# Out stage of a hybrid decoder layer: casts, low halves and sums of the output product ordered behind the newest convolution instruction of their engine

## The chip, the cores and the metric

The kernel runs on 1 core of one Trainium2 chip. The metric is the device time of the whole program in microseconds; each measurement is one execution, and the time before is the median of 3 of them. The core's engines are named as the profile names them: PE (matrix products), DVE, ACT and POOL (element-wise work), SP (issues DMAs); each works off its own stream of instructions in the order in which the compiler put them.

## What is computed

One layer of a decoder over 2048 prompt tokens and 8 x 4 sample tokens. Four branches of 512 channels each (convolution, pooling mixer, stick-breaking attention, attention into a memory) are gated, put side by side and multiplied by `w_out`; a norm, the residual and a final norm follow. The change touches the last part, which the reference writes so:

```python
def conv_branch(a, b, hist, w_dw, b_dw, ln_g, ln_b, w_pw, b_pw):
    ...
    y = y + b_dw                          # depthwise convolution
    y = jax.nn.silu(layer_norm(y, ln_g, ln_b))
    y = y @ w_pw + b_pw
    return y, u_ext[:, -(CONV_K - 1):]

mix = jnp.concatenate([y_c * jax.nn.silu(cg), y_p * jax.nn.silu(pg),
                       y_s * jax.nn.silu(sg), y_m * jax.nn.silu(mg)], axis=-1)
out = rms_norm(mix @ w_out, post_g)
return x + out, conv_new, pool_new, k, v
```

## The kernel before

The kernel first projects the tokens, runs the sample group's attention and the depthwise convolution, then the attention of the prompt. What is left at about 1960 us is the **out stage**, in which two streams of work are woven together.

The first is the **output product** `mix @ w_out`, 2048 x 2048 by 2048 x 1024. It is done as seven block products (a scheme of the Strassen kind, products 1, 7, 2, 6, 4, 5, 3 in this order), each of which is cut into parts `(prod, i, h)`: 128 tokens of sums or differences of `mix` rows against a half `h` of the block's weights. fp32 values are split into a high and a low half that PE can take: `hi` is a cast (ACT) and `lo = value - hi` (DVE or POOL). A part is therefore 12 matmuls (line 1968): for each of four slices of 128 rows `mh x wohi`, `mh x wolo`, `ml x wohi`. The helpers of a part: `out_load` (SP issues the DMA of rows into `mr`), `out_combine` (sums or differences of rows on POOL, lines 1698, 1701 and 1705, and on DVE, line 1704), `out_high` (ACT cast `mr` -> `mh`, line 1713), `out_low` (DVE `ml`, line 1724), and for the weights `weight_high` (ACT cast `wor` -> `wohi`, line 1620) and `weight_low` (`wolo`, line 1625). `lows(...)` asks for a part's `ml` in the second of the four steps of the part three places ahead of it (`AHEAD = 4`, `LOWK = 1`).

The second stream is `conv_post`, the **rest of the convolution branch**, eight blocks of 256 tokens, named by their first token (0, 256, 512 ... 1792). A block goes through a long chain from engine to engine:

- `total`: POOL adds four channel groups to `cs` (line 1442)
- `center`: PE `cm` (mean, line 1447), DVE `cy` (line 1450), ACT `csq` (squares, line 1452), POOL adds of `csq` (line 1454)
- `scale`: PE `cv` (variance, line 1460), ACT square root (line 1461), DVE reciprocal (line 1462), then twice, for two of the four channel groups: DVE `ct` (line 1469), ACT sigmoid `csg` (line 1472), DVE `ct` (line 1476), ACT `shi` (line 1478), DVE `slo` (line 1481). Square root and sigmoid need different tables in ACT, which an ACT_TABLE_LOAD loads
- `point`: PE `cz` (line 1502), four times 12 matmuls on `shi` and `slo`, with a DVE `cgt` (line 1505) and a store of the rows of `mix` after each

`conv` is advanced by one step whenever the loop over the parts has made 0.9 of a step (`OPACE`), so both streams are traced interleaved, and products 2 and 6 take the rows that the convolution writes.

PE's instruction order is fixed to the order of the program text, by `tc.manual_schedule` for PE. On DVE, ACT and POOL the order is chosen by the scheduler of the framework: an instruction may stand ahead of one that was traced earlier, where its operands come sooner. `tc.issue_after(x)` adds an edge to what is traced inside it: the instruction is not put ahead of `x`. It carries no data.

## Time and profile before

| | us |
|---|---|
| median of 3 runs | 2381.64 (2380.49 to 2384.3) |
| the profiled execution, whole time | 2378.62 |
| its span in the profile | 2376.9 |
| PE busy in the span | 2279.8 (96%) |
| DVE busy | 1720.7 (72%) |
| POOL busy | 1277.5 (54%) |
| ACT busy | 1119.1 (47%) |

The granted clock of the core is 0.989 on average. The out stage with the convolution in it lies between about 1960 and 2180 us; what follows to the end has output product and norms alone. A row of the timeline is: start in us, duration in us, engine, line, operation, out <- in, shapes, how many in the row, and in brackets the idle time ahead of it on its engine with what ended it. A row of the table by windows has for each engine the busy time and, in brackets, the instructions, and then PEclk (the clock granted to PE, 1.00 is full speed), the share of DMA time and GB/s.

### The profile page before, as it was taken

The page shows a single profiled execution, that of the slowest core. Times are in us where ns is not written, and L with a number is a line of the kernel's source. Part 1 is how long each engine was busy: PE and PEld are TensorE (multiplying, and loading weights), DVE is VectorE, ACT ScalarE, POOL GpSimd, SP SyncE. Part 2 cuts the span into 40 slices and gives each one's busy share as a digit, 9 for nine tenths or more (in the row PEclk, how much of TensorE's full clock was granted, in tenths as well). Part 3 has the DMA queues.
Part 4 walks back from the last instruction along what each step waited for, and adds up shares of the span by engine and source line. Part 5 has one row for each costly group of instructions (what it writes and reads, how often), then busy time and mean ns, then how long its engine had stood idle before and what let it go on. Part 6 is the DMA issues. An engine that isn't in the chain of part 4 may idle for free. (4 is left out here: it accounts for less than half of the span.)

```text
span 2376.9 us, 42227 instructions
## 1 busy us (share of the span) xinstructions
PE 2279.8 (96%) x16024; PEld 1772.0 (75%) x16024; DVE 1720.7 (72%) x2428; ACT 1119.1 (47%) x1947; POOL 1277.5 (54%) x1322
## 2 busy tenths in 40 slices
PE   7999999999999999999999999899999999999996
PEld 7898888888888777777777777555555557778775
DVE  5342786969557673577777877978898956777897
ACT  5322342242442322224242425788999965444554
POOL 3554546455565546445555552799877754432230
PEclk9999999999999999999999999999999999999998
DMA  6689977878778999887877775566442207866674
GB/s 213 194 282 299 336 270 261 281 259 276 256 257 311 321 346 344 308 289 267 299 262 269 262 264 154 143 214 216 111 107 72 76 23 249 265 210 196 233 236 158
DMA packets 336868, 557.94 MB, mean 235 GB/s; under 512 B 27985, under 2 KB 212433, under 8 KB 320266
## 3 DMA queue, kind: packets, MB, share of 16 engines
q1 hardware_dynamic: 281290, 286.53, 38.8%
q0 software_dynamic: 55376, 268.72, 31.9%
q8 instruction: 126, 2.06, 0.4%
q14 instruction: 76, 0.62, 0.1%
HBM read 465.09 MB, written 90.68 MB: 234 GB/s over the span
## 5 line engine op out<-in xcount | busy, mean ns | idle before, releaser
L966 DVE STREAM_TRANSPOSE T<-kt 128x1024 f32<-128x1024 f32 x256 | 308.7, 1226 | 190.4 <-PE sSA L979 177.3
L933 POOL DMA_INDIRECT vt<-in_cache_v_dram,idv x256 | 252.4, 986 | 260.0 <-PE sO L1018 199.0
L618 DVE SCALAR_TENSOR_TENSOR cacc<-U,par,cacc 128x512 f32<-128x512 f32 x480 | 359.9, 750 | 11.0
L1344 POOL TENSOR_TENSOR be<-be,E 128x512 f32<-128x512 f32 (+3 forms) x316 | 300.7, 963 | 67.4 <-DVE E L1332 23.7
L1335 DVE TENSOR_TENSOR_SCAN E<-gam,cr,ZM 128x513 f32<-128x513 f32 x192 | 233.3, 1264 | 21.6 <-ACT gam L1266 13.5
L933 POOL DMA_INDIRECT kt<-in_cache_k_dram,idk x128 | 128.5, 1004 | 195.0 <-DVE T L966 153.2
L1355 PEld LDWEIGHTS AT<-ident,be 128*128 128x128 f32 x1082 | 117.3, 142 | 136.5 <-ACT at L1361 40.6
L1968 PE MATMUL acc<-wohi,mh 128*128 128x512 f32 (+1 forms) x480 | 193.3, 403 | 0.5 <-DVE mh L1724 0.5
L1266 ACT ACTIVATE gam<-S,nbias_bc 128x1024 f32<-128x1024 f32 (+1 forms) x158 | 170.2, 1077 | 45.3 <-ACT be L1267 15.1
L1968 PE MATMUL acc<-wolo,mh 128*128 128x512 f32 (+1 forms) x480 | 189.4, 395 | 0.0
L1968 PE MATMUL acc<-wohi,ml 128*128 128x512 f32 x448 | 177.6, 396 | 5.4 <-DVE ml L1724 5.4
L1262 PE MATMUL S<-kT,Q 128*128 128x512 f32 (+1 forms) x632 | 175.8, 401 | 4.8 <-ACT be L1267 4.8
L1355 PE MATMUL AT<-ident,be 128*128 128x128 f32 x1082 | 160.4, 284 | 20.6 <-DVE at L1359 8.7
L1267 ACT ACTIVATE be<-S,bias_bc 128x1024 f32<-128x1024 f32 (+1 forms) x158 | 169.1, 1070 | 0.4 <-DMA gsd<-sg1sg 0.4
L1371 PE MATMUL av<-at,V 128*64 128x512 f32 (+3 forms) x640 | 152.8, 557 | 3.9 <-DVE sbo L1376 3.9
L979 PE MATMUL sSA<-T,W 128*32 128x128 f32 x4096 | 139.8, 276 | 2.7 <-DVE T L966 1.4
L979 PEld LDWEIGHTS sSA<-T,W 128*32 128x32 f32 x4096 | 105.1, 109 | 37.6 <-issue 31.2
L1018 PE MATMUL sO<-vt,saT 128*32 128x512 f32 x1024 | 122.2, 592 | 0.0
L1262 PEld LDWEIGHTS S<-kT,Q 128*128 128x128 f32 x632 | 106.1, 195 | 18.4 <-ACT be L1267 5.8
L1361 ACT COPY at<-AT 128x512 f32<-128x512 f32 x192 | 108.9, 651 | 19.7 <-PE AT L1355 19.6
L1332 DVE TENSOR_TENSOR_SCAN E<-gam,ZM 128x384 f32<-128x384 f32 (+1 forms) x124 | 94.5, 811 | 32.0 <-ACT gam L1266 26.3
L1724 DVE TENSOR_TENSOR ml<-mr,mh 128x512 fp32r<-128x512 f32 x108 | 91.0, 849 | 30.8 <-ACT mh L1713 30.6
(577 smaller groups left out, 6030.2 us busy)
## 6 DMA issues: line engine op xcount, KB each, us to landing
Q<-qd SPq DMA_DIRECT2D x64, 256.0 KB
mr<-mixd SPq DMA_DIRECT2D x32, 512.0 KB
mr<-mixd SPq DMA_DIRECT2D x48, 256.0 KB
xtp<-in_x_prompt_dram SPq DMA_DIRECT2D x16, 512.0 KB
kT<-kd SPq DMA_DIRECT2D x64, 128.0 KB
ws<-in_w_out_dram SPq DMA_DIRECT2D x16, 512.0 KB
wsd<-ws SPq DMA_DIRECT2D x16, 512.0 KB
msd<-mr SPq DMA_DIRECT2D x32, 256.0 KB
```

Source lines behind the costliest of these rows:

```text
L618: dve.scalar_tensor_tensor(out=ps, in0=U[:, a + k : a + k + H], scalar=wd[:, k : k + 1], in1=ps, op0=ALU.mult, op1=ALU.add)
L933: pool.indirect_dma_start(out=dst, out_offset=None, in_=rows, in_offset=bass.IndirectOffsetOnAxis(ap=idx, axis=0))
L966: S["turn"] = dve.transpose(T[:, 2 * hh : 2 * hh + 2].rearrange("p s j t -> p (s j t)"), kt[:, 2 * hh : 2 * hh + 2].rearrange("p s j d -> ...
L979: pe.matmul(sSs[n][32 * g : 32 * g + 32, P * ml : P * (ml + 1)], lhsT=W[:, jj, :], rhs=T[:, :, jj, :], start=i == 0, stop=i == 3, tile_pos ...
L1262: pe.matmul(S[:, j, :w], lhsT=Q[:, x, P * (q2 + j) : P * (q2 + j + 1)], rhs=kt[:, :w], start=x == 0, stop=x == 1)
L1266: act.activation(out=ga, in_=S[:, :, :w], func=AF.Sigmoid, bias=nbias_bc[:, h : h + 1], scale=-1.0)
L1267: act.activation(out=be, in_=S[:, :, :w], func=AF.Sigmoid, bias=bias_bc[:, h : h + 1])
L1335: dve.tensor_tensor_scan(out=E[:, j][:, ::-1], data0=g_[:, j][:, ::-1], data1=ZM[:, 0:1].to_broadcast([P, 513]), initial=carry[hh, q2][:, ...
L1344: pool.tensor_tensor(out=be[:, j, :m], in0=be[:, j, :m], in1=E[:, j, 513 - w : 513 - w + m], op=ALU.mult)
L1355: pe.transpose(ap_[:, P * qt : P * (qt + 1)], A[hp, qb, kc, hh, qt][:, P * r : P * (r + 1)], ident)
L1371: pe.matmul(av[64 * hh : 64 * hh + 64, c], lhsT=V[:, 4 * kc + r, 64 * hh : 64 * hh + 64], rhs=ats.pop((hp, qb, kc, r, hh))[:, c], start=dg ...
L1968: pe.matmul(o[:rows], lhsT=m[a][:, k, :rows], rhs=W[prod, 4 * h + k][w], start=not cont and h == k == n == 0, stop=h == 1 and k == 3 and n ...
```

## The change

`mark()` remembers, for ACT, DVE and POOL apart, the newest instruction of `conv_post` that has been traced. `behind_conv(eng)` wraps an instruction of the output product in `tc.issue_after` of that one. So each cast, low half, sum and difference of rows and weights in the out stage is no longer put ahead of convolution work that was traced before it on the same engine. Nothing is added to or taken from the computation, and the DMAs' and PE's code is untouched. Before the first marked instruction `latest` is empty, and nothing is wrapped.

```diff
+    latest = {}
+
+    def mark(x):
+        latest[x.ins.engine] = x.ins
+        return x
+
+    def behind_conv(eng):
+        x = latest.get({id(act): mybir.EngineType.Activation, id(dve): mybir.EngineType.DVE,
+                        id(pool): mybir.EngineType.Pool}[id(eng)])
+        return tc.issue_after(x) if x is not None else ExitStack()
...
@@ scale (so marked: every ACT, DVE and POOL instruction of total, center, scale and point)
-            dve.reciprocal(out=vps[:, :N], in_=vps[:, :N])
+            mark(dve.reciprocal(out=vps[:, :N], in_=vps[:, :N]))
...
@@ weight_high, weight_low
-        act.copy(hi, ts[0])
+        with behind_conv(act):
+            act.copy(hi, ts[0])
...
-        eng.tensor_tensor(out=lo, in0=raw_, in1=hi.bitcast(F32), op=ALU.subtract)
+        with behind_conv(eng):
+            eng.tensor_tensor(out=lo, in0=raw_, in1=hi.bitcast(F32), op=ALU.subtract)
...
@@ out_combine (so too its other sums, on POOL and DVE)
-            pool.tensor_tensor(out=ts[0], in0=ts[0], in1=ts[1], op=ALU.subtract)
+            with behind_conv(pool):
+                pool.tensor_tensor(out=ts[0], in0=ts[0], in1=ts[1], op=ALU.subtract)
...
@@ out_high
-        act.copy(mh[:, :, :rows], raws[x])
+        with behind_conv(act):
+            act.copy(mh[:, :, :rows], raws[x])
...
@@ out_low
-        eng.tensor_tensor(out=lo, in0=raw_, in1=hi.bitcast(F32), op=ALU.subtract)
+        with behind_conv(eng):
+            eng.tensor_tensor(out=lo, in0=raw_, in1=hi.bitcast(F32), op=ALU.subtract)
```

On PE no instruction moves. On the others the instructions of the out stage change places. Two places show how. The names in the rows carry the block or the part: `ct768_2` is channel group 2 of convolution block 768, `ml7_5_0` the low half of part (7, 5, 0); the number behind is a running one. In the changed kernel line 1713 has become 1720, 1724 has become 1732, 1756 has become 1764, and 1620 has become 1621.

DVE before, at the variance of convolution block 768, from the end of the block before to the first `slo`:

```order
L1724 TENSOR_TENSOR ml7_5_0_21063<-mr7_5_0_20898,mh7_5_0_21062 128x512
L1505 SCALAR_TENSOR_TENSOR cgt512_3_20976<-cz512_3_20996,par_116,cgt512_3_20976 128x256
L1756 TENSOR_TENSOR U3_20131<-acc7_3_20948,U2_20130 128x512
L1462 RECIPROCAL cv768_21032<-cv768_21032 128x256
L1724 TENSOR_TENSOR ml7_5_1_21108<-mr7_5_1_20942,mh7_5_1_21107 128x512
L1469 SCALAR_TENSOR_TENSOR ct768_0_21042<-cy768_20565,par_116,cv768_21032 128x256
L1469 SCALAR_TENSOR_TENSOR ct768_1_21046<-cy768_20565,par_116,cv768_21032 128x256
L1450 TENSOR_TENSOR cy1024_20821<-cy1024_20821,cm1024_21115 128x256 x4
L1476 SCALAR_TENSOR_TENSOR ct768_0_21042<-ct768_0_21042,par_116,csg768_0_21044 128x256
L1476 SCALAR_TENSOR_TENSOR ct768_1_21046<-ct768_1_21046,par_116,csg768_1_21048 128x256
L1756 TENSOR_TENSOR U3_20131<-acc7_4_21065,U2_20130 128x512
L1481 TENSOR_TENSOR slo768_21041<-ct768_0_21042,shi768_21040 128x256
```

The same place after the change; the reciprocal, `ml7_4_1` and `ct768_0` of line 1469 stand just ahead of the first row:

```order
L1469 SCALAR_TENSOR_TENSOR ct768_1_21046<-cy768_20565,par_116,cv768_21032 128x256
L1450 TENSOR_TENSOR cy1024_20821<-cy1024_20821,cm1024_21115 128x256 x4
L1476 SCALAR_TENSOR_TENSOR ct768_0_21042<-ct768_0_21042,par_116,csg768_0_21044 128x256
L1476 SCALAR_TENSOR_TENSOR ct768_1_21046<-ct768_1_21046,par_116,csg768_1_21048 128x256
L1764 TENSOR_TENSOR U3_20131<-acc7_4_21065,U2_20130 128x512
L1481 TENSOR_TENSOR slo768_21041<-ct768_0_21042,shi768_21040 128x256
L1481 TENSOR_TENSOR slo768_21041<-ct768_1_21046,shi768_21040 128x256
L1469 SCALAR_TENSOR_TENSOR ct768_2_21071<-cy768_20565,par_116,cv768_21032 128x256
L1469 SCALAR_TENSOR_TENSOR ct768_3_21075<-cy768_20565,par_116,cv768_21032 128x256
L1476 SCALAR_TENSOR_TENSOR ct768_2_21071<-ct768_2_21071,par_116,csg768_2_21073 128x256
L1476 SCALAR_TENSOR_TENSOR ct768_3_21075<-ct768_3_21075,par_116,csg768_3_21077 128x256
L1732 TENSOR_TENSOR ml7_5_0_21063<-mr7_5_0_20898,mh7_5_0_21062 128x512
```

`ml7_5_0` stood three rows ahead of the reciprocal; it now stands behind the second pair of line 1476, so that the reciprocal, eight `ct`, four `cy` and two `slo` stand ahead of it. `ml7_5_1`, which followed the reciprocal, now follows the last `slo` of the block.

ACT before, between the square root and the sigmoid of convolution block 512:

```order
L1713 CAST mh7_2_0_20795<-mr7_2_0_20637 128x512
L1461 ACT_TABLE_LOAD
L1461 ACTIVATE cv512_20765<-cv512_20765,eps_t_93 128x256
L1713 CAST mh7_2_1_20836<-mr7_2_1_20693 128x512
L1713 CAST mh7_3_0_20876<-mr7_3_0_20746 128x512
L1620 CAST wohi2_4_21139<-wor2_4_20915 128x512
L1620 CAST wohi2_5_21178<-wor2_4_20915 128x512
L1472 ACT_TABLE_LOAD
L1472 ACTIVATE csg512_0_20777<-ct512_0_20775,par_116 128x256
L1472 ACTIVATE csg512_1_20781<-ct512_1_20779,par_116 128x256
```

The same place after the change:

```order
L1720 CAST mh7_1_1_20750<-mr7_1_1_20617 128x512
L1461 ACT_TABLE_LOAD
L1461 ACTIVATE cv512_20765<-cv512_20765,eps_t_93 128x256
L1472 ACT_TABLE_LOAD
L1472 ACTIVATE csg512_0_20777<-ct512_0_20775,par_116 128x256
L1472 ACTIVATE csg512_1_20781<-ct512_1_20779,par_116 128x256
L1478 CAST shi512_20773<-ct512_0_20775 128x256
L1478 CAST shi512_20773<-ct512_1_20779 128x256
L1720 CAST mh7_2_0_20795<-mr7_2_0_20637 128x512
L1472 ACTIVATE csg512_2_20806<-ct512_2_20804,par_116 128x256
```

The weight casts `wohi2_4` and `wohi2_5` and two row casts no longer stand between square root and sigmoid; `mh7_2_0` has moved from ahead of the square root to behind the first two `shi`.

More of the change, by code (lines that the diff above doesn't have):

```diff
@@ L1441, in total @@
                 for c in range(3):
-                    pool.tensor_tensor(out=sums[i], in0=sums[i] if c else ys[i][:, 0, :N], in1=ys[i][:, c + 1, :N], op=ALU.add)
+                    mark(pool.tensor_tensor(out=sums[i], in0=sums[i] if c else ys[i][:, 0, :N], in1=ys[i][:, c + 1, :N], op=ALU.add))
         def center(i):
@@ L1449, in center @@
             for c in range(4):
-                dve.tensor_tensor(out=y[:, c, :N], in0=y[:, c, :N], in1=mps[:, :N], op=ALU.subtract)
+                mark(dve.tensor_tensor(out=y[:, c, :N], in0=y[:, c, :N], in1=mps[:, :N], op=ALU.subtract))
                 sq.append(cp.tile([P, CW], F32, tag="csq", name=f"csq{a0}_{c}", bufs=4)[:, :N])
-                act.activation(out=sq[c], in_=y[:, c, :N], func=AF.Square)
+                mark(act.activation(out=sq[c], in_=y[:, c, :N], func=AF.Square))
             for a, b in ((0, 1), (2, 3), (0, 2)):
-                pool.tensor_tensor(out=sq[a], in0=sq[a], in1=sq[b], op=ALU.add)
+                mark(pool.tensor_tensor(out=sq[a], in0=sq[a], in1=sq[b], op=ALU.add))
             sqs[i] = sq[0]
@@ L1460, in scale @@
             pe.matmul(vps[:, :N], lhsT=ones_ln, rhs=sqs.pop(i), start=True, stop=True)
-            act.activation(out=vps[:, :N], in_=vps[:, :N], func=AF.Sqrt, bias=eps_t)
-            dve.reciprocal(out=vps[:, :N], in_=vps[:, :N])
+            mark(act.activation(out=vps[:, :N], in_=vps[:, :N], func=AF.Sqrt, bias=eps_t))
+            mark(dve.reciprocal(out=vps[:, :N], in_=vps[:, :N]))
             yield
@@ L1468, in scale @@
                     t = ps_(f"ct{a0}_{c}")[:, :N]
-                    dve.scalar_tensor_tensor(out=t, in0=y[:, c, :N], scalar=par[:, c, CONV_K + 1 : CONV_K + 2],
-                                             in1=vps[:, :N], op0=ALU.mult, op1=ALU.mult)
+                    mark(dve.scalar_tensor_tensor(out=t, in0=y[:, c, :N], scalar=par[:, c, CONV_K + 1 : CONV_K + 2],
+                                                  in1=vps[:, :N], op0=ALU.mult, op1=ALU.mult))
                     sg = cp.tile([P, CW], F32, tag="csq", name=f"csg{a0}_{c}", bufs=4)[:, :N]
-                    act.activation(out=sg, in_=t, func=AF.Sigmoid, bias=par[:, c, CONV_K + 2 : CONV_K + 3])
+                    mark(act.activation(out=sg, in_=t, func=AF.Sigmoid, bias=par[:, c, CONV_K + 2 : CONV_K + 3]))
                     ts[c] = t, sg
@@ L1475, in scale @@
                 for c, (t, sg) in ts.items():
-                    dve.scalar_tensor_tensor(out=t, in0=t, scalar=par[:, c, CONV_K + 2 : CONV_K + 3], in1=sg,
-                                             op0=ALU.add, op1=ALU.mult)
-                    act.copy(shi[:, c, :N], t)
+                    mark(dve.scalar_tensor_tensor(out=t, in0=t, scalar=par[:, c, CONV_K + 2 : CONV_K + 3], in1=sg,
+                                                  op0=ALU.add, op1=ALU.mult))
+                    mark(act.copy(shi[:, c, :N], t))
                 yield
                 for c, (t, _) in ts.items():
-                    dve.tensor_tensor(out=slo[:, c, :N], in0=t, in1=shi[:, c, :N].bitcast(F32), op=ALU.subtract)
+                    mark(dve.tensor_tensor(out=slo[:, c, :N], in0=t, in1=shi[:, c, :N].bitcast(F32), op=ALU.subtract))
             split[i] = shi, slo
@@ L1504, in point @@
                         n += 1
-                dve.scalar_tensor_tensor(out=g[:, :N], in0=ps[:, :N], scalar=par[:, co, CONV_K + 3 : CONV_K + 4],
-                                         in1=g[:, :N], op0=ALU.add, op1=ALU.mult)
+                mark(dve.scalar_tensor_tensor(out=g[:, :N], in0=ps[:, :N], scalar=par[:, co, CONV_K + 3 : CONV_K + 4],
+                                              in1=g[:, :N], op0=ALU.add, op1=ALU.mult))
                 wq.dma_start(mix_rows(co, a0, CB), by_tile(g[:, :CB]))
@@ L1697, in out_combine @@
         if prod == 5 and i < LAST:
-            pool.tensor_tensor(out=ts[1], in0=ts[0], in1=ts[1], op=ALU.add)
+            with behind_conv(pool):
+                pool.tensor_tensor(out=ts[1], in0=ts[0], in1=ts[1], op=ALU.add)
             ts = ts[1:]
         elif prod == 7:
-            pool.tensor_tensor(out=ts[0], in0=ts[0], in1=ts[1], op=ALU.subtract)
+            with behind_conv(pool):
+                pool.tensor_tensor(out=ts[0], in0=ts[0], in1=ts[1], op=ALU.subtract)
             stores.append(((0, i, h), msd[0, i, h], ts[0]))
         elif prod == 6:
-            dve.tensor_tensor(out=ts[0], in0=ts[0], in1=ts[1], op=ALU.subtract)
-            pool.tensor_tensor(out=ts[2], in0=ts[2], in1=ts[0], op=ALU.subtract)
+            with behind_conv(dve):
+                dve.tensor_tensor(out=ts[0], in0=ts[0], in1=ts[1], op=ALU.subtract)
+            with behind_conv(pool):
+                pool.tensor_tensor(out=ts[2], in0=ts[2], in1=ts[0], op=ALU.subtract)
             stores.append(((1, i, h), msd[1, i, h], ts[2]))
```

## The prediction

> **What bounds the kernel now.** I read the engines' busy time first, then what PE waits for in the out stage, then the clock by windows of 5 us, and last the timelines around two convolution blocks.

> ```profile
> span 2376.9 us, 42227 instructions
> PE 2279.8 (96%) x16024; PEld 1772.0 (75%) x16024; DVE 1720.7 (72%) x2428; ACT 1119.1 (47%) x1947; POOL 1277.5 (54%) x1322
> ```

> PE is busy 96% of the span, and its order does not change. So the change can only alter the time in which PE stands still or runs at a lower clock. These are PE's waits between 1960 and 2180 us (line waited in, whom it waits for, us in total, times, longest):

> ```profile
> PE cz L1502 <- ACT shi L1478: 9.6, 4, 4.0
> PE cz L1502 <- DVE slo L1481: 2.7, 6, 0.8
> PE acc L1968 <- DVE ml L1724: 1.9, 3, 0.8
> PE cz L1502 <- DVE cgt L1505: 1.7, 1, 1.7
> ```

> They add up to 15.9 us. Of these 14.0 are PE waiting for the convolution (`cz`), and only 1.9 are PE waiting for the low halves of the output product (`ml`). Some of the stalls also cost clock, as the windows show (PEclk is the third number from the end):

> ```profile
> 2005.00:2010.00 5.00, 1.78 (x11) 1.24 (x9) 1.64 (x5) 2.50 (x6) 0.99 (x1) 0.94 0.77 277
> 2010.00:2015.00 5.00, 4.16 (x15) 3.56 (x16) 3.84 (x9) 2.76 (x8) 3.31 (x3) 0.50 0.75 229
> 2015.00:2020.00 5.00, 5.00 (x29) 4.54 (x29) 1.12 (x3) 0.50 (x1) 4.59 (x6) 0.88 1.06 367
> 2040.00:2045.00 5.00, 3.57 (x11) 2.89 (x12) 4.79 (x8) 2.62 (x8) 4.92 (x5) 0.51 0.75 257
> 2045.00:2050.00 5.00, 5.00 (x29) 4.53 (x28) 4.12 (x5) 0.00 (x0) 4.84 (x5) 0.81 0.82 237
> 2120.00:2125.00 5.00, 3.01 (x13) 2.41 (x13) 4.40 (x11) 2.71 (x8) 2.32 (x3) 0.70 0.96 336
> 2125.00:2130.00 5.00, 5.00 (x22) 4.40 (x21) 3.72 (x7) 0.62 (x1) 3.92 (x5) 0.62 0.45 151
> ```

> Three times PE falls to about half clock after it has stood still. What that costs is the busy time times the share of the clock that is missing: 4.16 x 0.50 + 5.00 x 0.12 = 2.7 us the first time, 3.57 x 0.49 + 5.00 x 0.19 = 2.7 the second, 3.01 x 0.30 + 5.00 x 0.38 = 2.8 the third; 8.2 us in all. Waits and clock together are **24.1 us**, which is all that the change could win here.

> Why the convolution comes late is seen at block 512, on ACT and DVE:

> ```profile
> 2031.68 1.14 ACT L1620 CAST wohi<-wor 128x512 fp32r<-128x512 f32 x2 [3.24 <-DMA wor<-in_w_out_dram]
> 2032.84 1.28 ACT L1472 ACT_TABLE_LOAD   x1
> 2034.13 0.84 ACT L1472 ACTIVATE csg<-ct,par 128x256 f32<-128x256 f32 x2
> 2034.64 0.88 DVE L1476 SCALAR_TENSOR_TENSOR ct<-ct,par,csg 128x256 f32<-128x256 f32 x2 [3.50 <-ACT csg L1472]
> ```

> ACT waits 3.24 us for a weight DMA, casts, and only then gets to the sigmoid; DVE meanwhile stands still for 3.50 us. Weight casts which nothing needs soon stand ahead of a chain that PE is about to need. The change takes these out of the way; that is its gain.

> **The change part by part. The gain.** With `wohi2_4` and `wohi2_5` behind the sigmoids, the 3.24 us wait, the casts' 1.14 us and the like at the other blocks leave the chain. I also expect PE to come later to `cz` because of what follows, by some 4 us a block. Both together should end nearly all `cz` waits: 14.0 us, the 1.9 for `ml` being replaced by the term below, and the 8.2 us of clock. Gain 24.1, at least 15 if some `slo` and `cgt` waits and one low clock stay.

> **The loss.** The low halves that PE needs within the chain now stand behind it. Block 768 ran undisturbed before, so I cost it there. PE, DVE and ACT from the block's variance `cv` on:

> ```profile
> 2054.08 0.59 PE L1460 MATMUL cv<-csq,ones_ln 128*128 128x256 f32 x2
> 2061.95 0.40 PE L1968 MATMUL acc<-wohi,mh 128*128 128x512 f32 x1
> 2062.42 0.40 PE L1968 MATMUL acc<-wohi,ml 128*128 128x512 f32 x1
> 2054.72 0.45 ACT L1461 ACTIVATE cv<-cv,eps_t 128x256 f32<-128x256 f32 x1 [1.53 <-PE cv L1460]
> 2059.54 1.28 ACT L1472 ACT_TABLE_LOAD   x1 [0.19 <-DVE ct L1469]
> 2060.83 0.84 ACT L1472 ACTIVATE csg<-ct,par 128x256 f32<-128x256 f32 x2
> 2065.29 0.83 ACT L1472 ACTIVATE csg<-ct,par 128x256 f32<-128x256 f32 x2
> 2056.73 1.75 DVE L1462 RECIPROCAL cv<-cv 128x256 f32<-128x256 f32 x1
> 2058.39 0.67 DVE L1724 TENSOR_TENSOR ml<-mr,mh 128x512 fp32r<-128x512 f32 x1
> 2058.98 0.87 DVE L1469 SCALAR_TENSOR_TENSOR ct<-cy,par,cv 128x256 f32<-128x256 f32 x2
> 2060.05 1.42 DVE L1450 TENSOR_TENSOR cy<-cy,cm 128x256 f32<-128x256 f32 x4 [0.20 <-PE cm L1447]
> 2061.38 0.88 DVE L1476 SCALAR_TENSOR_TENSOR ct<-ct,par,csg 128x256 f32<-128x256 f32 x2
> 2062.89 0.76 DVE L1481 TENSOR_TENSOR slo<-ct,shi 128x256 fp32r<-128x256 f32 x2
> 2063.56 0.87 DVE L1469 SCALAR_TENSOR_TENSOR ct<-cy,par,cv 128x256 f32<-128x256 f32 x2
> 2064.34 0.69 DVE L1724 TENSOR_TENSOR ml<-mr,mh 128x512 fp32r<-128x512 f32 x1
> 2065.79 0.88 DVE L1476 SCALAR_TENSOR_TENSOR ct<-ct,par,csg 128x256 f32<-128x256 f32 x2 [0.77 <-ACT csg L1472]
> 2066.58 1.67 DVE L1724 TENSOR_TENSOR ml<-mr,mh 128x512 fp32r<-128x512 f32 x1
> 2068.17 0.74 DVE L1481 TENSOR_TENSOR slo<-ct,shi 128x256 fp32r<-128x256 f32 x2
> ```

> The matmul at 2061.95 opens accumulator `acc7_5`: it takes `mh7_5_0`, and two matmuls later, at 2062.42, PE takes `ml7_5_0`. That is 8.3 us after `cv`. After the change `ml7_5_0` stands behind the second pair of line 1476. This pair ended at 2065.79 + 0.88 = 2066.7. One `ml` (0.69 us, at 2064.34) leaves the chain ahead of it; the one behind the reciprocal is only exchanged for another. So the pair ends between 2066.0 and 2066.7, and the `ml` behind it takes 0.69 to 1.67 us (both durations are in the rows; the long ones are those beside POOL's work). So `ml7_5_0` is there at 2066.7 to 2068.4, 12.6 us or more after `cv` where PE wants it after 8.3: PE stands from 2062.4 on, for **4.3 to 6.0 us**. Its `mh7_5_0` is late as well, behind the first two `shi` on ACT, but less, so that adds nothing.

> The order shows the same at the other blocks: one low half that PE wants 7 to 8 us after `cv` stands behind the second `ct` pair or behind the last `slo` (about 0.7 us more, from the row at 2068.17). For blocks 0, 1536 and 1792 somewhat less stands ahead of it. For these I take 3 to 4 us, for the other five 4.3 to 5.7: 3 x 3.5 + 5 x 4.8 = **34.5 us** over eight blocks; ends 8 x 3.0 = 24 (ends of chains tighten everywhere) and 8 x 5.7 = 46.

> PE cannot make up for this: what it lacks is the next part in its fixed order. The helpers behind the late `ml` (`ml7_5_1` after the last `slo`, then `wolo`) have a part's 12 matmuls as cover, 2.8 us, which about holds; if that cover is gone, each costs the 0.69 us of one more `ml`, inside the upper end.

> **Clock.** The long waits ahead of the three low clocks:

> ```profile
> 2010.82 0.58 PE L1502 MATMUL cz<-shi,pwhi 128*128 128x256 f32 x1 [4.04 <-ACT shi L1478]
> 2040.65 0.58 PE L1502 MATMUL cz<-shi,pwhi 128*128 128x256 f32 x1 [3.29 <-ACT shi L1478]
> 2042.01 0.58 PE L1502 MATMUL cz<-slo,pwhi 128*128 128x256 f32 x1 [0.78 <-DVE slo L1481]
> 2122.31 0.58 PE L1502 MATMUL cz<-shi,pwhi 128*128 128x256 f32 x1 [1.67 <-ACT shi L1478]
> ```

> 4.04 us in one piece, 3.29 and 0.78 in two, and once only 1.67 us at the end of a stretch with several short waits. The new stalls lie at 3 to 5.7 us, so more than half should set it off: 4.5 times 2.7 = **12 us**, ends 1 x 2.7 and 8 x 2.7 = 22. [...]

> **Costed at nothing.** The weight casts and lows pushed back (`wohi`, `wolo`, 24 each): `wohi2_4` is cast at 2031.68, and at 2061.95 PE only opens `acc7_5`, ahead of product 2 by six parts of 2.8 us (twelve matmuls at the 0.235 us between 2061.95 and 2062.42), so product 2 cannot begin before 2078; these 46 us hide a delay of one or two chains (13 us each); if that cover were gone it would be one more stall of the kind above. POOL's sums (mean 1.49 us, row below) wait mostly for DMA and stand three parts ahead; behind POOL's `csq` sums they are a chain late at most, and SP's stores of their results with them. The DMA issues on SP keep their places but for buffers freed later.

> ```profile
> L1701 POOL TENSOR_TENSOR mr<-mr 128x512 f32<-128x512 f32 x16 | 23.7, 1488 | 42.4 <-DMA mr<-mixd 27.7 <-DVE ct L1476 6.2 <-DVE ml L1724 4.5
> ```

> Bounds for these together: 0 and 8 us. From the end of the convolution on, nothing is marked any more and the orders agree.

> **The sum** against the profiled execution, 2378.6 us: - 24.1 + 34.5 + 12 = +22.4, so 2401 us; that execution lies 3.0 us below the median of the runs (2381.64 - 2378.62), so **2404 us**, 0.9% slower.

> **The rivals.** *A, faster: the low halves are in time.* Place: DVE between the reciprocal and the second `ct` pair. If the chain from `cv` to that pair took less than the 8.3 us after which PE asks for `ml`, every stall would go: 2381.6 - 24.1 = 2358 us. For it: part of the chain is waiting (3.50 us at block 512, 1.53, 0.77 at 768), and ACT has fewer instructions in between. Against it: the chain's own work, each step waiting for the one before, is 0.59 + 0.45 + 1.75 + 0.87 + 1.28 + 0.84 + 0.88 + 0.76 + 0.87 + 0.83 + 0.88 + 0.69 = 10.7 us; overlap inside pairs can take 2 us off, not the rest. It decides at 8.3 us.

> *B, about even: one stall for the other.* The chain tightens to the low end, PE stands 3 us a block, below what costs clock: 2381.6 - 24.1 + 24 + 2.7 = 2384 us. For it: at 3 us a stall is shorter than the 4.04 and 3.29 + 0.78 us that were followed by low clock. Against it: a stall of 3 us needs the low half 11.3 us after `cv`, and block 768 showed 12.6.

> *C, longer: lateness adds up.* Each stall costs the full 5.7 and sets off half clock, since DVE's 0.69 us steps stretch to 1.67 beside POOL and the lows of the next part are late again: 2381.6 - 24.1 + 46 + 22 = 2425 us. For it: the row of 1.67 us stands just where the late `ml` now goes. Against it: 2.8 us per part let DVE catch up.

> That the change does not do what it says is out: the order shows the low halves moved at all eight blocks.

> **How the numbers follow.** Forecast 0.60, A 0.14, B 0.12, C 0.14. The predicted time is 2404. A measurement of this kernel can tell about 0.2% (4.8 us) from no change. A is faster; of B I count 0.08 as within 0.2% and 0.03 as slower, 0.01 as faster; the forecast and C are slower: faster 0.15, same 0.08, slower 0.77. The range goes from B's time less a little, 2382, to C's, 2425; A is left out, with a little of C. The forecast's own range is 2392 to 2416.

> **What would show it.** Right: PE's waits in the stage are headed by `acc <- DVE ml`, at 30 us or more, with about one long wait per convolution block; `cz <- ACT shi` is nearly gone; ACT's wait for the weight DMA no longer stands ahead of a sigmoid; half clock appears in four or five stretches. Wrong in the mechanism: `acc <- DVE ml` stays under 5 us and `cz` waits vanish (A), or `cz` waits remain (chain not freed). Wrong in size: many `ml` waits of about 3 us with full clock (B), or two long waits in each block, one per part (C). What would make it wrong outside this: PE waits for `mr` from a DMA, or for `wohi`.

## The result, and the profile after

| | us |
|---|---|
| after, median of 6 runs | 2405.34 (2396.78 to 2416.6) |
| before, median of 6 runs on the same chip | 2381.58 (2379.02 to 2388.68) |
| ratio | 1.0097, 95% interval 1.0072 to 1.0122 |
| predicted | 2404 (2382 to 2425) |

The change makes the kernel 1.0% slower. The profiled execution took 2416.6 us, the longest of the six, and its span is 38.0 us longer than the one of before (2414.9 against 2376.9). Not all of this is the change. The first matrix product of the convolution's last stage, ahead of anything that the change moves, came at 1930.83 before:

```profile
1930.83 0.70 PE L1447 MATMUL cm<-cs,ones_ln 128*128 128x256 f32 x2 [1.72 <-ACT at L1361]
```

and after:

```profile
1943.01 0.70 PE L1447 MATMUL cm<-cs,ones_ln 128*128 128x256 f32 x2 [1.72 <-ACT at L1361]
```

So 12.2 us were lost earlier. In the profiled executions of the eleven kernels of the experiments below the same product comes between 1926.21 and 1938.18, so such a shift belongs to the single execution. The remaining 25.8 us come from there on. PE's waits between 1975 and 2225 us, after (line waited in, whom it waits for, us in total, times, longest):

```profile
PE acc L1986 <- DVE ml L1732: 21.7, 9, 4.4
PE acc L1986 <- ACT mh L1720: 9.8, 6, 3.7
```

These two rows are the whole table. The three `cz` rows of before are gone, and in this window PE waits for nothing but the low halves and casts of the output product: 31.5 us, where in the same window of before it waited 15.0. One window from each stretch with a low clock, after (PEclk is the third number from the end):

```profile
1995.00:2000.00 5.00, 5.00 (x15) 3.87 (x14) 1.74 (x5) 2.31 (x7) 2.65 (x5) 0.57 0.64 198
2025.00:2030.00 5.00, 3.21 (x8) 1.82 (x9) 3.79 (x9) 3.84 (x11) 2.69 (x4) 0.66 0.81 236
2055.00:2060.00 5.00, 5.00 (x12) 3.94 (x13) 4.86 (x5) 2.53 (x5) 4.92 (x4) 0.50 0.98 358
2085.00:2090.00 5.00, 5.00 (x17) 3.92 (x17) 4.45 (x7) 2.75 (x7) 4.33 (x4) 0.70 0.96 297
2115.00:2120.00 5.00, 5.00 (x15) 3.93 (x16) 5.00 (x7) 4.71 (x10) 4.20 (x4) 0.63 0.35 113
2145.00:2150.00 5.00, 5.00 (x14) 3.92 (x13) 3.36 (x5) 1.25 (x3) 1.48 (x2) 0.55 0.75 250
2175.00:2180.00 5.00, 5.00 (x23) 4.16 (x22) 4.81 (x6) 1.93 (x4) 4.30 (x4) 0.82 0.14 52
2200.00:2205.00 5.00, 4.25 (x12) 3.40 (x13) 4.84 (x10) 3.33 (x8) 0.59 (x1) 0.66 0.29 67
```

There are eight such stretches, one for each block of the convolution, some 30 us apart. Busy time times missing clock, summed over all windows of 5 us from 1975 to 2225, is 15.5 us; before it is 8.3. Waits and clock together: 47.0 us after, 23.3 before, a difference of **23.7**. The medians differ by 23.8.

Block 768, whose cost the prediction worked out, looks like this after:

```profile
2072.65 0.59 PE L1460 MATMUL cv<-csq,ones_ln 128*128 128x256 f32 x2
2081.83 0.50 PE L1986 MATMUL acc<-wohi,mh 128*128 128x512 f32 x1 [1.13 <-ACT mh L1720]
2084.57 0.79 PE L1986 MATMUL acc<-wohi,ml 128*128 128x512 f32 x1 [2.01 <-DVE ml L1732]
2073.74 1.28 ACT L1472 ACT_TABLE_LOAD   x1
2081.16 0.62 ACT L1720 CAST mh<-mr 128x512 fp32r<-128x512 f32 x1
2081.36 0.74 DVE L1481 TENSOR_TENSOR slo<-ct,shi 128x256 fp32r<-128x256 f32 x2
2083.04 0.89 DVE L1476 SCALAR_TENSOR_TENSOR ct<-ct,par,csg 128x256 f32<-128x256 f32 x2 [0.15 <-ACT csg L1472]
2083.84 0.68 DVE L1732 TENSOR_TENSOR ml<-mr,mh 128x512 fp32r<-128x512 f32 x1
2085.04 0.75 DVE L1481 TENSOR_TENSOR slo<-ct,shi 128x256 fp32r<-128x256 f32 x2
```

`ml7_5_0` runs at 2083.84, right behind the second `ct` pair, as the order said. It is done 11.9 us after `cv`, and PE has waited 2.01 us for it after 1.13 us for its cast.

### The profile page after: what moved, and what is told of

It is laid out like the page before. It is cut to its first block, busy times and chain, and to the rows that moved or that the text cites. A ratio compares the mean times of both kernels' runs of the same rounds, so it can differ in the third digit from the quotient of the medians.

```text
span 2414.9 us, 42222 instructions
## 1 busy us (share of the span) xinstructions
PE 2296.5 (95%) x16024; PEld 1781.0 (74%) x16024; DVE 1715.1 (71%) x2428; ACT 1119.5 (46%) x1947; POOL 1273.9 (53%) x1322
## 5 line engine op out<-in xcount | busy, mean ns | idle before, releaser
L1986 PE MATMUL acc<-wohi,mh 128*128 128x512 f32 (+1 forms) x480 | 199.0, 415 | 10.5 <-ACT mh L1720 10.3
L1986 PE MATMUL acc<-wohi,ml 128*128 128x512 f32 x448 | 183.9, 411 | 26.3 <-DVE ml L1732 26.1
L1986 PEld LDWEIGHTS acc<-wohi,ml 128*128 128x128 f32 x448 | 87.7, 196 | 54.6 <-DVE ml L1732 35.0
L1986 PEld LDWEIGHTS acc<-wohi,mh 128*128 128x128 f32 (+1 forms) x480 | 92.3, 192 | 35.4 <-ACT mh L1720 13.6
```

What stands on the lines that cost most here:

```text
L1986: pe.matmul(o[:rows], lhsT=m[a][:, k, :rows], rhs=W[prod, 4 * h + k][w], start=not cont and h == k == n == 0, stop=h == 1 and k == 3 and n ...
```

## Experiments

All use the same program text; what differs is which of the wrapped instructions keep the wrap, or how old the convolution instruction is behind which they stand. In the table, "waits" is the sum of PE's waits from 1975 to 2225 us and "clock" the busy time times the missing clock there, both from the run's one profiled execution; the last column is their sum less the 23.3 us of before. The change of the median is the ratio's, times 2381 us.

| run | behind the convolution | ratio (95%) | us by ratio | waits | clock | less before |
|---|---|---|---|---|---|---|
| after | all | 1.0097 (1.0072 to 1.0122) | +23 | 31.5 | 15.5 | +23.7 |
| rows | casts mh, lows ml | 1.0186 (1.0150 to 1.0221) | +44 | 44.7 | 22.4 | +43.8 |
| lows | lows ml | 1.0169 (1.0145 to 1.0193) | +40 | 49.8 | 18.6 | +45.1 |
| casts | casts mh | 1.0104 (1.0080 to 1.0129) | +25 | 33.9 | 13.1 | +23.7 |
| sums | sums of rows | 0.9991 (0.9973 to 1.0008) | -2 | 14.3 | 5.8 | -3.2 |
| weights | wohi, wolo | 0.9985 (0.9969 to 1.0001) | -4 | 13.9 | 4.4 | -5.0 |
| lag4 | all, rows and sums 4 steps older | 1.0006 (0.9989 to 1.0023) | +1 | 18.4 | 3.1 | -1.8 |
| lag8 | all, rows and sums 8 steps older | 0.9962 (0.9944 to 0.9980) | -9 | 11.2 | 2.4 | -9.7 |
| lag8_w8 | all, everything 8 steps older | 0.9963 (0.9949 to 0.9976) | -9 | 10.9 | 2.6 | -9.8 |
| lag8_wfree | rows and sums 8 steps older | 0.9974 (0.9963 to 0.9984) | -6 | 13.6 | 6.1 | -3.6 |
| lag12 | all, rows and sums 12 steps older | 0.9947 (0.9932 to 0.9962) | -13 | 10.7 | 2.5 | -10.1 |

Over runs from -13 to +44 us, PE's waits and its missing clock in this stage account for the time to about 5 us, although waits and clock come from one execution each and the start of the stage shifts between executions.

**Which part costs.** Five runs keep the wrap on one kind of instruction each (rows: on casts and lows) and take it from the others, as here from the weight casts:

```diff
-        with behind_conv(act):
+        with ExitStack():
             act.copy(hi, ts[0])
```

> Only the weight casts and weight lows (wohi, wolo) stay behind the convolution; row casts, row lows and sums are free as before. Theory (the gain is the weights', the loss is the rows'): the waits of ACT for the weight DMA no longer stand in the convolution's chain, PE's cz waits fall from 14.0 us to 5 or less, at most one stretch of half clock is left, acc waits for ml stay at 3 us or less: about 2367 us (2360 to 2374). Rival (the convolution is late because of the row lows in its chain, not the weights): cz waits stay above 9 us, 2378 to 2384 us.

Measured 2375.05 us. PE's largest waits in this run from 1975 to 2225 us:

```profile
PE cz L1502 <- ACT shi L1478: 5.8, 5, 1.8
PE cz L1502 <- DVE slo L1481: 3.3, 7, 1.0
PE cz L1502 <- DVE cgt L1505: 2.6, 1, 2.6
PE acc L1986 <- ACT wohi L1621: 1.2, 1, 1.2
```

The time lies between the theory's range and the rival's; the waits are the rival's. The long waits for `shi` are gone (longest 1.8 instead of 4.0 us) and with them half of the lost clock, but 11.7 of the 14.0 us for `cz` stay. The weight casts made the convolution late in places; they are not most of its lateness. By time alone the run is not told apart from the kernel before, since its interval reaches 1.0001.

> Only the row casts and row lows (mh, ml) stay behind the convolution; weights and sums are free as before. Theory: the waits of acc for mh and ml are those of the full change (25 to 40 us, one long one per block) with half clock at six or more blocks, cz waits nearly vanish because PE comes later: 2400 to 2412 us. Rival one (the weights or sums made the loss): 2376 to 2386 us. Rival two (weights in the chain make the row lows later still): 2415 us or more.

Measured 2425.1 us: the loss is the rows', and rival two is right that it becomes larger without the weights' edge. The longest wait shows why, in the timeline of this run, on ACT, DVE and PE at block 512:

```profile
2037.41 1.14 ACT L1621 CAST wohi<-wor 128x512 fp32r<-128x512 f32 x2 [9.95 <-DMA wor<-in_w_out_dram]
2038.56 1.28 ACT L1461 ACT_TABLE_LOAD   x1
2039.86 0.45 ACT L1461 ACTIVATE cv<-cv,eps_t 128x256 f32<-128x256 f32 x1
2042.01 0.67 DVE L1732 TENSOR_TENSOR ml<-mr,mh 128x512 fp32r<-128x512 f32 x1
2042.74 0.80 PE L1986 MATMUL acc<-wohi,ml 128*128 128x512 f32 x1 [6.59 <-DVE ml L1732]
```

ACT waits 9.95 us for a weight that nothing needs yet, the square root stands behind it, the reciprocal behind that, the low half behind the reciprocal, and PE waits 6.59 us. A low half that stands behind the chain inherits whatever holds the chain.

> Only the row lows (ml) stay behind the convolution; row casts, weights and sums are free. Theory (it is the lows that come late, the casts are only late beside them): acc waits for ml of 25 us or more, half clock at five places or more, mh waits under 3 us, 2398 to 2425 us. Rival (the casts mh or the sums behind ACT's and POOL's convolution work are what is late): 2378 to 2392 us.

Measured 2422.39 us. The two longest waits, 10.21 us at block 256 and 9.81 at block 1280, have free instructions ahead of the chain. At block 256 a free row cast stands ahead of a sigmoid on ACT and waits 3.07 us for its sum. At block 1280 it is on DVE: a sum of rows waits for its DMA, the `ct` pair stands behind it, and PE waits 9.81 us (timeline of this run, DVE and PE):

```profile
2142.05 0.69 DVE L1709 TENSOR_TENSOR mr<-mr 128x512 f32<-128x512 f32 x1 [2.63 <-DMA mr<-msd]
2150.50 0.80 PE L1986 MATMUL acc<-wohi,ml 128*128 128x512 f32 x1 [9.81 <-DVE ml L1732]
```

> Only the row casts (mh) stay behind the convolution; lows, weights and sums are free. Each low needs its cast, and the cast stands behind the first two shi, so the low comes two thirds of a chain late instead of a whole one. Theory: acc waits for mh and ml together 8 to 20 us, 2383 to 2397 us. Rival (the casts alone make the whole loss): 2400 us or more. Rival two (they cost nothing): 2382 us or less.

Measured 2407.51 us, 10 us above the range: the first rival. The casts alone, with all else free, cost as much as the whole change; PE's largest waits, same window:

```profile
PE acc L1986 <- ACT mh L1720: 25.1, 10, 6.5
PE acc L1986 <- DVE ml L1732: 4.7, 8, 1.0
PE acc L1986 <- DVE mh L1732: 3.5, 1, 3.5
```

A cast need only stand behind the first two `shi` to be late, since PE takes it two matmuls ahead of the low half, and 25.1 us of waits follow. The low half is then late too, but PE has waited already. The chain is held up by free instructions here as well: ahead of the longest wait (6.46 us, block 1024) a free sum stands before the reciprocal on DVE and waits for its DMA:

```profile
2095.99 0.69 DVE L1709 TENSOR_TENSOR mr<-mr 128x512 f32<-128x512 f32 x1 [4.32 <-DMA mr<-msd]
```

So the costs of these runs do not add up to that of the full change, in which such instructions stand behind the chain too; what the casts cost within the full change is not shown.

> Only the sums and differences of rows (POOL, and one DVE step) stay behind the convolution. Theory: they have three parts of lead, PE's waits stay as before: 2377 to 2386 us. Rival (late sums make mh and ml late): acc waits for mh or ml of 8 us or more, 2390 us or more.

Measured 2379.11 us, as the theory said. PE's waits are 14.3 us in all as against 15.0, though 6.2 of them are now for `mh` and `ml`, under the rival's 8. In the full change ACT's casts do wait for these sums, as ACT's waits from 1975 to 2225 us show, but the sums alone lose nothing:

```profile
ACT mh L1720 <- POOL mr L1705: 18.9, 7, 3.9
```

**Is it the place or the lead?** In the program text a low half is asked for 20 matmuls of the output product ahead of its use, after the second step of the part two places ahead (not three, as said above): 1.7 parts. If the loss is the chain's length less this lead, then a wrap that looks a few steps back (a step is a quarter of a part) must take the loss away, though a low half still stands at the same place in DVE's order. `mark` now keeps a list with the step of the loop over the parts, and the wrap takes the newest entry that is old enough:

```diff
-        latest[x.ins.engine] = x.ins
+        latest.setdefault(x.ins.engine, []).append((now[0], x.ins))
...
-        x = latest.get({...}[id(eng)])
+        old = latest.get({...}[id(eng)], ())
+        x = next((i for t, i in reversed(old) if t <= now[0] - lag), None)
...
             conv_due += 1.0
+            now[0] += 1
```

> The full change, but row casts, lows and sums stand only behind convolution instructions that were traced four or more steps of the loop over the parts earlier (weights as in the full change). In the order the low behind the second ct pair is then one part later in PE's stream: PE wants it about 10.6 us after cv instead of 7.8, and it comes at about 12.6. Theory (chain length minus lead is the stall): acc waits of about 8 to 16 us, one of 1 to 2 us per block, no half clock from them, 2373 to 2385 us. Rival (standing behind the convolution is what costs, whatever the lead): 2398 us or more.

> As before with eight steps: the low behind the second ct pair is one that PE wants about 14.9 us after cv and that comes at about 12.6, so it is in time. Theory: acc waits for ml and mh under 4 us, cz waits at most what they are with the weights alone behind (11.7 us), less since only one or two lows are left in the chain, 2366 to 2377 us, below the kernel before. Rival (the convolution's lateness in the kernel before has nothing to do with row casts and lows in its chain): as with the weights alone, 2375 us or more. Rival two (standing behind costs, whatever the lead): 2398 us or more.

Measured 2381.77 and 2372.54 us, both inside the theory's ranges and far from the 2398 us of the rival that the place costs. The waits for `ml` fall from 21.7 us to 13.5 at lag 4 and to none at lag 8. At lag 4 the theory missed in one place: block 1536 has a wait of 3.85 us, and half clock comes with it (PEclk 0.59 from 2140 us to 2145); the only other low clock of this run is at the start of the stage, up to about 1977. Lag 8 is only 2.5 us below the other rival (as with the weights alone), and the two intervals overlap; what speaks against it is the `cz` waits, 8.1 us instead of 11.7. At lag 8 block 768 reads so in DVE's timeline:

```profile
2056.62 0.88 DVE L1476 SCALAR_TENSOR_TENSOR ct<-ct,par,csg 128x256 f32<-128x256 f32 x2 [0.15 <-ACT csg L1472]
2057.41 0.68 DVE L1732 TENSOR_TENSOR ml<-mr,mh 128x512 fp32r<-128x512 f32 x1
2058.61 0.75 DVE L1481 TENSOR_TENSOR slo<-ct,shi 128x256 fp32r<-128x256 f32 x2
```

The picture is that of the changed kernel: a low half directly behind the second pair. But it is the one of the part after next, and no wait for a low half is left in the table of PE's waits:

```profile
PE cz L1502 <- DVE cgt L1505: 5.6, 2, 4.7
PE acc L1987 <- ACT mh L1720: 3.1, 1, 3.1
PE cz L1502 <- ACT shi L1478: 1.4, 1, 1.4
PE cz L1502 <- DVE slo L1481: 1.1, 2, 0.9
```

The waits for `shi` and `slo`, 12.3 us before, are 2.5; the 3.1 for `mh` lie 41 us after the `cv` of the last block. The run is faster than the kernel before (0.9944 to 0.9980): here it is a gain to stand behind the convolution, once the lead is as long as the chain.

> As lag8, but weight casts and lows too stand only behind convolution instructions of eight or more steps earlier. In lag8 seven weight lows came in a row behind slo of block 1024 and held the cgt that PE waited 4.7 us for. Theory (that pile-up is the price of the weights' edge to the newest instruction): the 4.7 us wait shrinks to under 2 us, 2364 to 2371 us. Rival (weights return into the chain): cz waits for shi and slo above 6 us, 2374 us or more.

> As lag8, but weight casts and lows are free, as in the kernel before. Theory one (the weights in the chain are part of why the convolution came late): cz waits for shi and slo return, ACT waits for the weight DMA ahead of a sigmoid return, 2374 to 2384 us, slower than lag8 by 3 us or more. Theory two (the gain of lag8 is that of row casts and lows alone): 2366 to 2374 us, as lag8.

Measured 2371.91 and 2374.29 us. The first was a miss: the longest `cgt` wait is 3.4 us, not under 2, the `cgt` waits are 5.4 us in all against 5.6, and the intervals are nearly the same, so the row of weight lows is not shown to be the price. The second lies between its theories: rows and sums alone bring about two thirds of lag8's gain, but the intervals overlap.

> As lag8 with twelve steps: lows wanted some 20 us after cv are the first behind the chain, so two to three more lows and casts stand in it. Theory (each low in the chain delays shi and slo by about 0.7 us, a low behind it that is in time costs nothing): slower than lag8 and near the run with the weights alone behind, 2371 to 2378 us, cz waits 8 to 12 us. Rival (the lag does not matter once the lows are in time): 2366 to 2372 us.

Measured 2369.89 us, the fastest of all, with PE's largest waits:

```profile
PE cz L1502 <- DVE cgt L1505: 5.6, 3, 2.5
PE acc L1987 <- ACT wohi L1621: 2.1, 1, 2.1
PE cz L1502 <- DVE slo L1481: 1.9, 4, 0.9
PE acc L1987 <- DVE ml L1732: 0.9, 1, 0.9
```

The theory that more lows in the chain make it slower was a miss: `cz` waits are 7.5 us, not 8 to 12. The intervals of lag 8 and lag 12 overlap. **lag12 is faster than both kernels**; the gain on the one before is 0.5%.

**How much is the clock?** Nine matmuls without use are put ahead of each of six parts that wait:

```diff
+        if x in KEEP:
+            for _ in range(9):
+                pe.matmul(o[:rows], lhsT=W[prod, 0][0][:, :P], rhs=W[prod, 0][0], start=True, stop=True)
```

> The full change, with nine extra matmuls on PE (about 2.1 us, their result is overwritten) ahead of each of the six parts whose first low half comes late: (7,2,0), (7,5,0), (2,0,0), (6,1,0), (2,3,0), (6,4,0). Theory (a third of the loss is PE's clock, which falls after a long stall): the stalls become shorter than 3 us, half clock goes at these six places, 2395 us (2391 to 2399), the sum of idle and extra matmuls staying what the idle was. Rival (the late halves alone set the time, the clock costs nothing that is not waited for anyway): 2403 to 2408 us. Rival two (the extra matmuls only delay PE): 2412 us or more.

Measured 2396.5 us (ratio 1.0075, 1.0049 to 1.0102). In its profile PE waits 20.3 us and the missing clock costs 5.8 instead of 15.5. The 54 extra matmuls take 54 x 0.235 = 12.7 us (nine of them took 2.07 us, from 2034.58 to 2036.65); waits and extra work, 33.0 us, are about the 31.5 us that the waits were. So about 10 us of clock went and little came in their place; half clock stays at two of the six places (blocks 512 and 1024: PEclk 0.67 from 2040 us to 2045 and 0.79 from 2095 to 2100). This holds for one profiled execution of each kernel. The time lies in the theory's range, but it falls by 0.2%, about half as much, and the two intervals overlap, so the runs do not yet confirm the size.

## Why the prediction was right

**The gain**, 24.1 us, happened: the `cz` waits and the three old stretches of low clock are gone. But its first reason carried less than the prediction gave it. The weights alone bring 5.0 us in the profile and 4 by the ratio, whose interval includes no gain. Most `cz` waits go for the second reason that it gave, because PE is held up elsewhere first: in the run with rows alone, where ACT still waits for weights, one `cz` wait is left:

```profile
PE cz L1502 <- DVE cgt L1505: 0.8, 1, 0.8
```

Where PE is not held up, as in lag8, 8.1 of the 14.0 us for `cz` are still there. So most of that gain is the loss in another row of the table, not something that the change earned.

**The loss** was put at 34.5 us, eight waits of 4.3; it is 31.5: 29.7 in the eight blocks, in the main one stall each, and 1.8 at the very start, 2 to 4 us after the first `cv`. The rule (chain length less lead) held, and lag4 and lag8 show it as a dose. Its terms were off. At block 768 the prediction had 4.3 to 6.0 us and the trace has 1.13 + 2.01. The low half was there 11.9 us after `cv` instead of 12.6 or more, and PE, without its wait for the cast, would have come to it after 8.8 us (2084.57 - 2.01 - 1.13 - 2072.65), not 8.3; the difference is the 3.1 us of the two waits. The second pair ended after 11.3 us instead of 11.9 to 12.6: with no row cast behind the square root, ACT loads the sigmoid's table at 2073.74, before the reciprocal begins on DVE at 2075.29, and the first `csg` no longer waits for it. The sign given, `acc <- DVE ml` at 30 us or more, came out as 21.7 us, since 9.8 stand under `mh`. At four blocks, 768 among them, PE waits for the cast and two matmuls later for the low half of the same part; there the stall ends with the low half, and "its `mh7_5_0` is late as well [...] so that adds nothing" is right. It does not hold everywhere: at block 256 the stall is a single wait of 3.72 us for `mh`, and the run with the casts alone shows that late casts can stop PE by themselves.

**The clock**: 4.5 drops of 2.7 us were predicted, 12 us; it is 15.5, in eight drops of 1.9 us.

**Costed at nothing**: the sums alone show no cost (0.9991, 0.9973 to 1.0008). Of the weights the same holds, with `lag12` and `weights` showing one wait of 2.1 and 1.2 us for a `wohi`.

**The sum**, 34.5 + 12 = 46.5, was met by 31.5 + 15.5 = 47.0: two errors of 3 us that cancel, so that the forecast came within 2 us of the median is in part luck.

**The rivals.** A named the point that decides, 8.3 us from `cv` to the low half; the low half came after 11.9 at block 768, so A fell. The low clock in all eight stretches speaks against B. C gave 2425 us for waits that set off the clock every time; the clock did fall every time, but the waits were shorter than C's. The runs with rows or lows alone reached C's time by another way, through what holds up the chain.

## What to carry to other kernels

Before an instruction is ordered behind a chain, compare two times: how long the chain runs until that point, and how long after the chain's start its reader comes. Where the lead is shorter, the reader waits for the difference once per chain, and it inherits every stall of the chain as well; an edge to an older instruction of the chain keeps the chain free without this. When one wait vanishes, check whether it was removed or whether the engine is merely late for another reason.

## What was not expected of the hardware

PE's clock fell after a wait that was much shorter than most of those that the prediction went by. After, at 2172 us, PE had been at work for 26 us since its last wait, waited once, and then ran at half clock for 3.4 us:

```profile
2172.43 0.50 PE L1986 MATMUL acc<-wohi,ml 128*128 128x512 f32 x1 [2.23 <-DVE ml L1732]
```

With lag 4, a wait of 2.28 us was followed by no drop:

```profile
2086.91 0.50 PE L1987 MATMUL acc<-wohi,ml 128*128 128x512 f32 x1 [2.28 <-DVE ml L1732]
```

The granted clock in the traces tells the two apart. Before, half clock begins at 2009.38, 2040.10 and 2122.02 us, 9 and 24 times 3.413 us from one to the next. After, its eight stretches begin whole multiples of 3.413 us apart, from 1992.45 to 2200.67, and last one or two of them. In all 13 profiled executions (before, after and the eleven of the experiments) the changes of the clock from 1975 us to 2225 fit such a grid of 3.413 us to 0.05 us; where the grid begins differs between executions. Windows cut along it read so after (the first number behind the comma is PE's busy time):

```profile
2169.95:2173.36 3.41, 1.18 (x6) 0.79 (x5) 3.41 (x10) 2.29 (x8) 0.30 (x1) 1.00 0.30 109
2173.36:2176.77 3.41, 3.41 (x10) 2.66 (x9) 3.38 (x7) 1.98 (x5) 2.40 (x4) 0.50 0.00 0
2176.77:2180.19 3.42, 3.42 (x20) 2.95 (x20) 3.23 (x5) 1.50 (x3) 2.79 (x3) 1.00 0.20 77
```

and so with lag 4:

```profile
2082.92:2086.33 3.41, 1.71 (x8) 1.09 (x6) 3.41 (x8) 2.77 (x9) 0.72 (x1) 1.00 0.47 143
2086.33:2089.75 3.42, 2.83 (x14) 2.38 (x15) 3.42 (x6) 3.42 (x9) 2.39 (x3) 1.00 0.53 177
2089.75:2093.16 3.41, 2.72 (x20) 2.25 (x20) 3.41 (x4) 1.61 (x4) 2.70 (x3) 1.00 0.59 176
```
